# A decoder layer on one Trainium2 core: two more pairs of blocks computed with seven products, and a convolution chain in the FFN moved two weight units earlier

## The chip, the cores and the metric

The kernel runs on one core of a Trainium2 chip. A core has five engines with a queue of instructions each: TensorE (PE in the profile) multiplies matrices, VectorE (DVE) and ScalarE (ACT) do elementwise work, GpSimd (POOL) and SyncE (SP) do little here but start DMA transfers. An engine runs its queue in order and waits on semaphores for the work of the others. The metric is the device time of one execution in microseconds, the median of several runs.

## The reference

A decoder layer, batch 1, 256 tokens, width 2048, all in float32, with 28 inputs:

```python
hn = rmsnorm(h, norm_mix_w)
q, k, v, g_ret, xr, yr, g_a, g_b = split(hn @ w_in)      # 1024,1024,2048,2048, then 4 x 2048
q = rotary(q); k = rotary(k) * 128**-0.5                  # 8 heads of 128
ret_out = silu(g_ret) * head_groupnorm(chunkwise_retention(q, k, v))   # 8 heads of 256 values
hr = rg_lru(causal_dwconv(xr));  rnn_out = gelu(yr) * hr
merged = sigmoid(g_a) * (ret_out @ w_proj_ret) + sigmoid(g_b) * (rnn_out @ w_proj_rnn)
h = h + merged @ w_mix_out
h = h + memory_cross_attention(rmsnorm(h), rmsnorm(mem))  # 4 heads of 512, 256 memory tokens
up = causal_dwconv(rmsnorm(h) @ ffn_w_up)                 # 2048 -> 11264, 3 taps
gate, val = split(up)
h = h + (silu(gate) * val) @ ffn_w_down                   # 5632 -> 2048
out = rmsnorm(h, final_norm_w)
```

Nearly all of the work is the products with the weights, some 420 MB of them, each used once.

## The kernel before

**Products.** Float32 operands are split into two parts, hi and lo, that TensorE multiplies fast; a product of two float32 matrices is hi·hi + lo·hi + hi·lo, three TensorE products.

**The weight stream.** `weight_plan` (L65) lists the products of the whole layer in the order in which they run, and the host lays the weights out in that order in `wall`, as pieces of 1 MB: 4 row tiles of 128 by 512 columns. A *unit* is one step of TensorE on one such piece. `prefetch` (L248) prepares a unit: SP loads the piece into one of 6 buffers `raw` (L265), ScalarE casts hi (L286), VectorE takes lo = raw - hi (L287); hi and lo have 3 buffers each. `units` (L308) keeps two units prepared ahead of the one that runs. After each unit it runs the small work that has been put off by `later(n, fn)` (L304): n + 1 steps on from where it was registered. The Tile scheduler then writes out each engine's order from these program positions; blocks under `tc.high_priority(URGENT)` go ahead of their place.

**Three ways to run a block of 512 columns.** `gemm_t` (L328) keeps the weights stationary and gives features by tokens, in two accumulators; `joined` (L539) empties them (ScalarE copy L544, VectorE add L545). `gemm_n` (L371) streams the weights and gives tokens by features in one accumulator, 96 products of TensorE for 16 row tiles (L362, L363, L369). `pair_products` (L385) does two neighbouring blocks at once with seven products instead of eight (Strassen-Winograd): eight of the sixteen row tiles go through the seven units q1 to q7 of 12 products each, the rest through the plain units p0 to p3 of 24 each, 180 products in place of 192. It takes all three accumulators of the pool `pm` (xz, yu, rw). The sums of weights that it needs are made in the raw buffers, three of which it names A, B and C: q5 and q7 by an adding DMA of GpSimd (L267: A gets another piece added, later B does), and two VectorE adds (L294: A + B behind q5's lo; L292: A + C behind the lo of the unit that follows q6). q6 and q4 cast what stands in A and load nothing. The order of the units is `PAIR_UNITS` (L103): q1, p0, q3, p1, q5, q2, q6, p2, q7, q4, p3. The sums of the activations are made by `sums` (L494); `pair_out` (L445) and `pair_add` (L424) take the results out of the accumulators.

**The front.** The weight plan begins with Q, V, K, V (blocks of 512 columns each), then the retention gate as a pair; then the second half of the heads, with its two value blocks as a pair. The input, transposed by the host (`x_t`), is loaded, scaled and split while Q runs (`Pairs`, L618). The four sums for the pairs need x_t again: `sum_x` (L867) loads a tile (L870), scales it on ScalarE (L872) and makes the sums; it is called at steps 0 to 3 behind the first value block. `tables` (L691), one step behind Q, makes the rotary tables and spreads the row factors over the partitions (through TensorE, L605); `rotated` (L713) turns Q and K. `split_rows` scales and splits the value blocks.

**The FFN** runs in three parts of 4, 4 and 3 column blocks of hidden features. A block takes a gate and a value product (`up`, L1261): gemm_n, then ScalarE writes 16-bit planes, SP starts two DMA transposes (`turn_planes`, L1201; L1205), ScalarE joins the planes (`join_planes`, copies L763) and VectorE scales; `conv` (L1277) is one ScalarE and two VectorE instructions per tile of 128 features, the taps; `hidden` (L1351) makes silu(gate)·value and splits it. Each of these chains has two halves (pr = 0, 1), put off by `at` steps: (1, 2) for most blocks, (2, 4) for the last value block of parts one and two. The last value block of part three runs as gemm_t instead (`at=None`), and so needs no transpose. Then come the down products into the residual rows `hrow`: parts one and two as two pairs (`pair_add`), part three as four blocks (`down`, L1288) of 12 row tiles, the last of them split in four quarters with the final norm behind each. The sums of activations are made only for the first four halves of a paired part (L1358). SP also keeps the residual rows in DRAM between parts (`put_rows`, `get_rows`) and loads the final norm's weights (L1383).

Of the kernel before, what the change touches and what calls it, by code (L numbers as in the profile page):

```python
# [14 lines left out]
ALU = mybir.AluOpType  # L15
# [49 lines left out]
def weight_plan():  # L65

    w0 = "w_in"
    plan = []
    v, u = O_V, O_V + 1024
    plan += [(w0, 0, NT, O_Q), (w0, 0, NT, v), (w0, 0, NT, O_K), (w0, 0, NT, v + BW), (w0, 0, NT, O_G, O_G + BW)]  # L70
    plan += [(w0, 0, NT, O_Q + BW), (w0, 0, NT, u, u + BW), (w0, 0, NT, O_K + BW)]
    plan += [(w0, 0, NT, O_G + 1024, O_G + 1024 + BW)]
    for b in range(4):
        plan += [(w0, 0, NT, c + b * BW) for c in (O_XR, O_YR)]
    for w, c, pairs in ((w0, O_GA, (0, 2)), (w0, O_GB, (0,)), ("w_proj_ret", 0, (0, 2))):
        plan += [(w, 0, NT, c + b * BW, c + (b + 1) * BW) for b in pairs]
        if len(pairs) == 1:
            plan += [(w, 0, NT, c + b * BW) for b in (2, 3)]
    plan += [("w_proj_rnn", 0, NT, b * BW) for b in range(4)]
    plan += residual_plan("w_mix_out")  # L80
    plan += [(w, 0, NT, b * BW, (b + 1) * BW) for w in ("xa_w_q", "xa_w_k") for b in (0, 2)]
    plan += residual_plan("xa_w_v")
    plan += residual_plan("xa_w_o")
    b0 = 0
    for nb_ in FF_PARTS:
        for b in range(b0, b0 + nb_):
            plan += [("ffn_w_up", 0, NT, c + b * BW) for c in (0, FF)]
        if nb_ == 4:
            plan += [("ffn_w_down", b0 * BW, NT, b * BW, (b + 1) * BW) for b in (0, 2)]
        else:  # L90
            plan += [("ffn_w_down", b0 * BW, 4 * nb_, b * BW) for b in range(4)]
        b0 += nb_
    return plan

# [20 lines left out]
]  # L115


def entry_units(e):

    w, row, nk, cols = e[0], e[1], e[2], e[3:5]  # L120
    if len(cols) == 1:
        return [("p", None, "new", (w, tuple(row + (k + i) * P for i in range(KC)), cols[0])) for k in range(0, nk, KC)]
    out = []
    for kind, slot, a in PAIR_UNITS:
# [30 lines left out]
def hybrid_layer(  # L155
# [148 lines left out]
    def later(n, fn):  # L304

        pending.append((step[0] + n + 1, fn))
# [75 lines left out]
                lower_n(a[:, tt, :], ops[tt], parts, k0 + KC >= nk)  # L382
        return a

    def pair_products(w, row, st, ss, c0, c1, out):  # L385
# [19 lines left out]
        e = (w, row, NT, c0, c1)  # L405
# [18 lines left out]
    def pair_add(w, row, st, ss, c0, c1, h0, h1):  # L424

        def add(o, i, op=ALU.add):
            dve.tensor_tensor(out=o, in0=o, in1=i, op=op)  # L427

        def out(kind, x, z, yu, rw):
            if kind == "q1":  # L430
                add(h0[:, 0, :], x)
            elif kind == "q5":
                later(3, lambda: add(h1, rw))
                later(4, lambda: add(h1, z[:, None, :].to_broadcast([P, 2, BW])))
            elif kind == "q6":
                add(h1[:, 0, :], x, ALU.subtract)
            elif kind == "q7":
                add(h0[:, 1, :], x)
                add(h1[:, 1, :], x, ALU.subtract)
            elif kind == "p3":  # L440
                add(h0, yu)

        pair_products(w, row, st, ss, c0, c1, out)

    def pair_out(w, st, ss, c0, r=None):  # L445

# [435 lines left out]
    for g in range(2):  # L882
        dec = big([P, 4, S], s="dec")
        vs, turned = [], []
        for b, o in enumerate((O_Q, O_K)):
            a = qjoin if g == b == 0 else [joined(t, "q") for t in gemm_t("w_in", 0, xs, NT, o + g * BW)]
            if b == 0:
                sp.dma_start(
                    out=dec,
                    in_=consts[:, C_DEC + g * 4 * S : C_DEC + (g + 1) * 4 * S].rearrange("p (h s) -> p h s", s=S),  # L890
                )
            if g > 0:
                turned.append(rotated(a))
                if b == 0:
                    vs += [split_rows(v, rs0) for v in pair_out("w_in", xs, xs_sums, O_V + 1024)]
            else:
                if b == 1:
                    turned.append(rotated(a))
                v = gemm_n("w_in", 0, xs, NT, O_V + b * BW)
                if b == 0:  # L900
# [360 lines left out]
    def up(c0, b, at, then):  # L1261

        if at is None:
            for pr, a in enumerate(gemm_t("ffn_w_up", 0, h2s, NT, c0 + b * BW)):
                then(pr, scaled(a, "uz"))
            return
        d = turn_planes(row_planes(gemm_n("ffn_w_up", 0, h2s, NT, c0 + b * BW)))

        def turned(pr):
            z = join_planes(d, pr)  # L1270
            dve.tensor_tensor(out=z, in0=z, in1=rsb2, op=ALU.mult)
            then(pr, z)

        for pr in range(2):
            later(at[pr], lambda pr=pr: turned(pr))
# [72 lines left out]
            hrow[b] = big([P, 2, BW], s="nat")  # L1348
            sp.dma_start(out=hrow[b], in_=fkept[n, b])

    def hidden(gt, vl, pr, summed):  # L1351
# [11 lines left out]
    for part, nb_ in enumerate(FF_PARTS):  # L1363
# [3 lines left out]
        for b in range(b0, b0 + nb_):  # L1367
# [6 lines left out]
            def finish_up(pr, z, b=b, gt=gt, vl=vl, paired=paired):  # L1374
                conv(FF, b, pr, z, vl)
                hidden(gt, vl, pr, paired)
# [56 lines left out]
```

## Time and profile before

| | |
|---|---|
| median of 3 runs | 1997.59 us (1996.73 to 1998.44) |
| the profiled execution, its own time | 1995.6 us |
| its span, first to last instruction | 1993.8 us |
| TensorE busy | 1968.6 us (99%), 9304 products |
| VectorE busy | 1566.4 us (79%) |
| ScalarE busy | 1277.2 us (64%) |
| GpSimd busy | 43.2 us (2%) |
| mean granted TensorE clock | 0.995 |
| moved by DMA | 456.59 MB, mean 229 GB/s |

The profile is of one execution, which lies 2.0 us below the median. PE is TensorE's products, PEld its weight loads, which overlap them; a queue's own steps carry a q (SPq). "L287 DVE ... lo<-raw,hi x420 | 950.9, 2267" is a group of instructions: line 287, on VectorE, writing lo from raw and hi, 420 of them, 950.9 us in all, 2267 ns each; what follows is the idle time of the engine just ahead of them and what ended it. The granted clock is the share of full speed at which TensorE ran in a stretch. A page of averages says little about single places, so most of the reading is of stretches of 2 to 40 us.

### The profile page before, as it was taken

To read this page: it belongs to the slowest core of one execution; us is meant where nothing else is said; L and a number is where in the kernel's file an instruction comes from. 1 tells how busy PE (TensorE), PEld (TensorE's weight loads), DVE (VectorE), ACT (ScalarE), POOL (GpSimd) and SP (SyncE) were. 2 spreads that over 40 slices of the span, in tenths; PEclk is the share of its full clock that TensorE was granted. 3 is DMA by queue.
4 is the path that set the end of the run, shared out by engine and by line. 5 is a ranking of instruction groups with operands and counts; after the bars stand their busy time and mean duration, and the time that the engine had idled before them with its cause. 6 is when DMAs were issued, how large, how long until landed. Compare 5 with 4: busy or idle time off the path is not lost.

```text
span 1993.8 us, 23634 instructions
## 1 busy us (share of the span) xinstructions
PE 1968.6 (99%) x9304; PEld 1650.8 (83%) x9304; DVE 1566.4 (79%) x1546; ACT 1277.2 (64%) x1323; POOL 43.2 (2%) x52
## 2 busy tenths in 40 slices
PE   9999999999999999999999999999989999899998
PEld 7888888888888888888888888888878888788887
DVE  6978888889886886779988778677786777885775
ACT  6655656767677554567778756567744667546662
POOL 0000000000000000000000000000000000000000
PEclk9999999999999999999999999999999999899999
DMA  9675674655887865878998748766777677686671
GB/s 369 233 261 147 223 264 161 230 190 160 266 260 220 248 250 190 252 256 258 270 259 235 267 125 271 236 226 204 234 232 273 207 219 236 204 278 228 211 245 61
DMA packets 146463, 456.59 MB, mean 229 GB/s; under 512 B 77744, under 2 KB 82480, under 8 KB 98608
## 3 DMA queue, kind: packets, MB, share of 16 engines
q1 hardware_dynamic: 139072, 410.51, 58.7%
q0 software_dynamic: 5760, 41.95, 11.6%
q10 hardware_dynamic: 1520, 2.63, 0.4%
q8 instruction: 73, 1.20, 0.2%
q14 instruction: 38, 0.31, 0.0%
HBM read 420.96 MB, written 16.78 MB: 220 GB/s over the span
## 4 chain that ended last, share of the span: by engine, by line
PE 91%; DVE 4%; ACT 2%; DMA 1%; issue 1%; SPq 0%; POOLq 0%; ACTq 0%; DVEq 0%
PE acc L362 25%; PE acc L363 25%; PE acc L369 24%; PE acc L351 14%; PE sm L518 2%; DVE lo L287 1%; ACT hi L286 1%; DMA raw<-in_wall 1%; PE acc L518 1%; PE sm L948 1%; PE sm L532 1%; DVE raw L294 0%; DVE fv L1283 0%; DMA d<-rp 0%; DVE tb L722 0%
## 5 line engine op out<-in xcount | busy, mean ns | idle before, releaser
L287 DVE TENSOR_TENSOR lo<-raw,hi 128x2048 fp32r<-128x2048 f32 (+1 forms) x420 | 950.9, 2267 | 297.8 <-ACT hi L286 297.0
L286 ACT CAST hi<-raw 128x2048 fp32r<-128x2048 f32 (+1 forms) x418 | 793.2, 1901 | 522.7 <-PE acc L363 374.8
L362 PE MATMUL acc<-hi,s 128*128 128x512 f32 x2008 | 787.3, 392 | 12.4 <-ACT hi L286 12.3
L363 PE MATMUL acc<-hi,s 128*128 128x512 f32 x2008 | 784.3, 391 | 0.0
L369 PE MATMUL acc<-lo,s 128*128 128x512 f32 x2008 | 501.1, 389 | 0.0
L362 PEld LDWEIGHTS acc<-hi,s 128*128 128x128 f32 x2008 | 378.6, 189 | 91.5 <-ACT hi L286 13.2
L363 PEld LDWEIGHTS acc<-hi,s 128*128 128x128 f32 x2008 | 378.9, 189 | 78.5 <-DVE s L556 1.0
L369 PEld LDWEIGHTS acc<-lo,s 128*128 128x128 f32 x2008 | 377.1, 188 | 78.3
L351 PE MATMUL acc<-s,hi 128*128 128x512 f32 x832 | 200.4, 392 | 2.1 <-DVE hi L284 1.5
L351 PEld LDWEIGHTS acc<-s,hi 128*128 128x128 f32 x832 | 153.5, 188 | 32.8 <-issue 1.6
L362 PE MATMUL acc<-hi,ss 128*128 128x512 f32 x320 | 125.8, 393 | 0.8 <-ACT o L454 0.6
L363 PE MATMUL acc<-hi,ss 128*128 128x512 f32 x320 | 124.7, 390 | 0.0
L763 ACT COPY jp<-d 128x512 uint16<-128x512 uint16 x132 | 93.4, 771 | 29.4 <-DMA d<-rp 29.3
L351 PEld LDWEIGHTS acc<-s,lo 128*128 128x128 f32 x832 | 107.1, 191 | 4.9 <-DVE lo L287 1.3
L351 PE MATMUL acc<-s,lo 128*128 128x256 f32 x832 | 110.5, 284 | 0.5 <-DVE lo L287 0.5
L369 PE MATMUL acc<-lo,ss 128*128 128x512 f32 x320 | 85.6, 389 | 0.0
L362 PEld LDWEIGHTS acc<-hi,ss 128*128 128x128 f32 x320 | 60.1, 188 | 14.5 <-ACT o L454 1.4
L369 PEld LDWEIGHTS acc<-lo,ss 128*128 128x128 f32 x320 | 60.1, 188 | 12.6
L363 PEld LDWEIGHTS acc<-hi,ss 128*128 128x128 f32 x320 | 60.1, 188 | 12.2
L267 POOL DMA_DIRECT2D raw<-in_wall x40 | 35.2, 880 | 1550.7 <-DVE lo L287 887.5
L427 DVE TENSOR_TENSOR nat<-nat,acc 128x512 f32<-128x512 f32 (+1 forms) x49 | 44.0, 910 | 14.9 <-PE acc L369 14.9
L292 DVE TENSOR_TENSOR raw<-raw,raw 128x2048 f32<-128x2048 f32 x20 | 45.8, 2288 | 0.4
(235 smaller groups left out, 1251.7 us busy)
## 6 DMA issues: line engine op xcount, KB each, us to landing
raw<-in_wall SPq DMA_DIRECT2D x333, 1024.0 KB, 5.0
raw<-in_wall POOLq DMA_DIRECT2D x40, 1024.0 KB, 8.2
fkept<-nat SPq DMA_DIRECT2D x12, 512.0 KB, 7.7
nat<-fkept SPq DMA_DIRECT2D x12, 512.0 KB, 5.6
xt<-in_x_t SPq DMA_DIRECT2D x11, 256.0 KB, 7.8
raw<-in_wall SPq DMA_DIRECT2D x5, 512.0 KB, 7.9
nat<-in_x ACTq DMA_DIRECT2D x4, 512.0 KB, 10.1
ret<-hr SPq DMA_DIRECT2D x4, 512.0 KB, 4.6
```

The source lines that it names most:

```text
L267: pool.dma_start(out=raw, in_=src, accum_op=ALU.add)
L286: act.copy(hi[:, a:b], raw[:, a:b])
L287: dve.tensor_tensor(out=lo[:, a:b], in0=raw[:, a:b], in1=hi[:, a:b].bitcast(F32), op=ALU.subtract)
L292: dve.tensor_tensor(out=to, in0=to, in1=by, op=ALU.add)
L351: pe.matmul(a, part, sx, start=k == 0 and t == 0, stop=k == nk - 1 and t == 0, skip_group_check=True)
L362: pe.matmul(o, h, hi, start=start and kk == 0, stop=False, skip_group_check=True)
L363: pe.matmul(o, l, hi, start=False, stop=False, skip_group_check=True)
L369: pe.matmul(o, h, lo, start=False, stop=stop and kk == KC - 1, skip_group_check=True)
L427: dve.tensor_tensor(out=o, in0=o, in1=i, op=op)
L518: ins = pe.matmul(o, a, b, start=start and i == 0, stop=stop and i == 2, skip_group_check=True)
L532: ins = pe.transpose(t[:, j, tt * P : (tt + 1) * P], rows[:, tt, k + j * P : k + (j + 1) * P], ident)
L763: ins = act.copy(words(t)[:, :, :, 1 - i], d[:, i, 2 * pr : 2 * pr + 2, :])
```

## The change

Three parts, in one diff.

1. The first two value blocks of the front become a pair of seven products, and the order of the plan becomes Q, K, value pair, gate pair. `sum_x` is now called at steps 0 to 3 behind Q, that is during K; Q is rotated at step 1 and K at step 8 of what follows, during the value pair. The load of the decay tables `dec` moves ahead of the block.
2. The first two down blocks of the FFN's last part become a pair too. They have 12 row tiles, so eight go through q1 to q7 and four through p0 and p1 only, in an order of their own (`SHORT_PAIR_UNITS`); the two blocks' results are finished together behind it. The sums of activations are now made in this part too. Blocks 2 and 3 stay as they were.
3. In parts one and two the last value block's halves both run two steps behind the block, in place of two and four, and their whole chain (join, scale, convolution, hidden, sums) is under high priority.

```diff
@@ weight_plan
-    plan += [(w0, 0, NT, O_Q), (w0, 0, NT, v), (w0, 0, NT, O_K), (w0, 0, NT, v + BW), (w0, 0, NT, O_G, O_G + BW)]
+    plan += [(w0, 0, NT, O_Q), (w0, 0, NT, O_K), (w0, 0, NT, v, v + BW), (w0, 0, NT, O_G, O_G + BW)]
...
-            plan += [("ffn_w_down", b0 * BW, 4 * nb_, b * BW) for b in range(4)]
+            plan += [("ffn_w_down", b0 * BW, 4 * nb_, 0, BW)]
+            plan += [("ffn_w_down", b0 * BW, 4 * nb_, b * BW) for b in (2, 3)]
+SHORT_PAIR_UNITS = [
+    ("q1", "A", ("new", 0, 0)),
+    ("q3", "B", ("new", 1, 1)),
+    ("q2", "C", ("new", 1, 0)),
+    ("p0", None, (1, 8)),
+    ("q5", "A", ("add", 0, 1)),
+    ("p1", None, (0, 8)),
+    ("q6", "A", ("sum",)),
+    ("q7", "B", ("add", 0, 1)),
+    ("q4", "A", ("sum",)),
+]
@@ pair_add (nk is passed on to pair_products)
+            short = nk < NT
             if kind == "q1":
                 add(h0[:, 0, :], x)
             elif kind == "q5":
-                later(3, lambda: add(h1, rw))
-                later(4, lambda: add(h1, z[:, None, :].to_broadcast([P, 2, BW])))
+                later(0 if short else 3, lambda: add(h1, rw))
+                later(1 if short else 4, lambda: add(h1, z[:, None, :].to_broadcast([P, 2, BW])))
...
-            elif kind == "p3":
+            elif kind == ("q4" if short else "p3"):
                 add(h0, yu)
@@ the front, for g in range(2)
-        for b, o in enumerate((O_Q, O_K)):
-            a = qjoin if g == b == 0 else [joined(t, "q") for t in gemm_t("w_in", 0, xs, NT, o + g * BW)]
...
-            if g > 0:
-                turned.append(rotated(a))
-                if b == 0:
-                    vs += [split_rows(v, rs0) for v in pair_out("w_in", xs, xs_sums, O_V + 1024)]
-            else:
-                if b == 1:
-                    turned.append(rotated(a))
-                v = gemm_n("w_in", 0, xs, NT, O_V + b * BW)
-                if b == 0:
-                    turned.append(rotated(a))
-                    for i in range(KC):
-                        later(i, lambda i=i: sum_x(i))
-                vs.append(split_rows(v, rs0))
...
+        if g == 0:
+            for i in range(KC):
+                later(i, lambda i=i: sum_x(i))
+            for n, a in ((1, qjoin), (8, block(O_K))):
+                later(n, lambda turned=turned, a=a: turned.append(rotated(a)))
+            value_rows()
+        else:
+            turned.append(rotated(block(O_Q)))
+            value_rows()
+            turned.append(rotated(block(O_K)))
@@ up
         def turned(pr):
-            z = join_planes(d, pr)
-            dve.tensor_tensor(out=z, in0=z, in1=rsb2, op=ALU.mult)
+            with tc.high_priority(URGENT if at[0] == at[1] else 0):
+                z = join_planes(d, pr)
+                dve.tensor_tensor(out=z, in0=z, in1=rsb2, op=ALU.mult)
             then(pr, z)
@@ the FFN
-        if summed and len(hid_sums) < KC:
+        if len(hid_sums) < KC:
             hid_sums.append(sums(o, 0.5))
...
-            up(FF, b, None if last and not paired else (2, 4) if last else (1, 2), finish_up)
+            def finish_last(pr, z, finish_up=finish_up):
+                with tc.high_priority(URGENT):
+                    finish_up(pr, z)
+
+            if last and paired:
+                up(FF, b, (2, 2), finish_last)
+            else:
+                up(FF, b, None if last else (1, 2), finish_up)
...
-            for b in range(4):
+            pair_add("ffn_w_down", b0 * BW, hid, hid_sums, 0, BW, hrow[0], hrow[1], 4 * nb_)
+            for b in range(2):
+                finish(b)
+            for b in (2, 3):
                 down(b0, hid, b, final)
```

More of the change, by code (lines that the diff above doesn't have):

```diff
@@ L123, in entry_units @@
     out = []
-    for kind, slot, a in PAIR_UNITS:
+    for kind, slot, a in PAIR_UNITS if nk == NT else SHORT_PAIR_UNITS:
         if kind[0] == "p":
@@ L383, in gemm_n, with pair_products @@
         return a
-    def pair_products(w, row, st, ss, c0, c1, out):
+    def pair_products(w, row, st, ss, c0, c1, out, nk=NT):
         xz, yu, rw = acc(), acc(), acc()
@@ L404, in pair_products @@
         names = {"q1": "x", "q2": "y", "q3": "r", "q4": "u", "q5": "z", "q6": "x", "q7": "x"}
-        e = (w, row, NT, c0, c1)
+        e = (w, row, nk, c0, c1)
         for kind, parts in units(*e):
@@ L422, in pair_products, with pair_add @@
                 out(kind, x, z, yu, rw)
-    def pair_add(w, row, st, ss, c0, c1, h0, h1):
+    def pair_add(w, row, st, ss, c0, c1, h0, h1, nk=NT):
         def add(o, i, op=ALU.add):
@@ L439, in out @@
                 add(h1[:, 1, :], x, ALU.subtract)
-            elif kind == "p3":
+            elif kind == ("q4" if short else "p3"):
                 add(h0, yu)
-        pair_products(w, row, st, ss, c0, c1, out)
+        pair_products(w, row, st, ss, c0, c1, out, nk)
     def pair_out(w, st, ss, c0, r=None):
@@ L884, in hybrid_layer, with block, value_rows @@
         vs, turned = [], []
-        for b, o in enumerate((O_Q, O_K)):
-            a = qjoin if g == b == 0 else [joined(t, "q") for t in gemm_t("w_in", 0, xs, NT, o + g * BW)]
-            if b == 0:
[L888 to L891, printed above, removed]
-            if g > 0:
-                turned.append(rotated(a))
-                if b == 0:
-                    vs += [split_rows(v, rs0) for v in pair_out("w_in", xs, xs_sums, O_V + 1024)]
-            else:
-                if b == 1:
-                    turned.append(rotated(a))
-                v = gemm_n("w_in", 0, xs, NT, O_V + b * BW)
-                if b == 0:
-                    turned.append(rotated(a))
-                    for i in range(KC):
-                        later(i, lambda i=i: sum_x(i))
-                vs.append(split_rows(v, rs0))
+        sp.dma_start(
+            out=dec,
+            in_=consts[:, C_DEC + g * 4 * S : C_DEC + (g + 1) * 4 * S].rearrange("p (h s) -> p h s", s=S),
+        )
+        def block(o):
+            return [joined(t, "q") for t in gemm_t("w_in", 0, xs, NT, o + g * BW)]
+        def value_rows():
+            vs.extend(split_rows(v, rs0) for v in pair_out("w_in", xs, xs_sums, O_V + g * 1024))
+        if g == 0:
[8 more added lines that the diff above has]
+            turned.append(rotated(block(O_K)))
         qr, kr = turned
@@ L1349, in get_rows, with hidden @@
             sp.dma_start(out=hrow[b], in_=fkept[n, b])
-    def hidden(gt, vl, pr, summed):
+    def hidden(gt, vl, pr):
         cs = slice(2 * pr, 2 * pr + 2)
@@ L1372, in hybrid_layer, with finish_up @@
                 later(0, lambda part=part, n=2 if paired else 4: get_rows(part % 2, range(n)))
-            def finish_up(pr, z, b=b, gt=gt, vl=vl, paired=paired):
+            def finish_up(pr, z, b=b, gt=gt, vl=vl):
                 conv(FF, b, pr, z, vl)
-                hidden(gt, vl, pr, paired)
-            up(FF, b, None if last and not paired else (2, 4) if last else (1, 2), finish_up)
+                hidden(gt, vl, pr)
+            def finish_last(pr, z, finish_up=finish_up):
[5 more added lines that the diff above has]
+                up(FF, b, None if last else (1, 2), finish_up)
         if final:
```

## The prediction

> **What bounds the kernel now.** I read the page's first and fifth parts, then stretches whose ends I set where TensorE changes from one weight block to the next, then the waits, the chain and the timeline at the four places that the change touches.
>
> ```profile
> span 1993.8 us, 23634 instructions
> PE 1968.6 (99%) x9304; PEld 1650.8 (83%) x9304; DVE 1566.4 (79%) x1546; ACT 1277.2 (64%) x1323; POOL 43.2 (2%) x52
> L287 DVE TENSOR_TENSOR lo<-raw,hi 128x2048 fp32r<-128x2048 f32 (+1 forms) x420 | 950.9, 2267 | 297.8 <-ACT hi L286 297.0
> L286 ACT CAST hi<-raw 128x2048 fp32r<-128x2048 f32 (+1 forms) x418 | 793.2, 1901 | 522.7 <-PE acc L363 374.8
> ```
>
> TensorE sets the time; each unit of 1 MB of weights also costs ScalarE 1.9 us (hi cast) and VectorE 2.3 us (lo).
>
> ```profile
> core 0: us, PE busy (x) PEld busy (x) DVE busy (x) ACT busy (x) POOL busy (x), PEclk, DMA share, GB/s
> 30.28:52.55 22.27, 22.27 (x103) 18.48 (x101) 15.33 (x22) 14.94 (x23) 0.71 (x1) 1.00 1.00 401
> 52.55:74.77 22.22, 22.22 (x130) 19.69 (x129) 20.66 (x28) 13.89 (x18) 0.00 (x0) 1.00 0.79 306
> 74.77:96.55 21.78, 21.78 (x98) 18.03 (x97) 19.00 (x25) 13.22 (x15) 1.04 (x1) 1.00 0.46 148
> 96.55:137.35 40.80, 40.80 (x181) 33.79 (x180) 33.71 (x20) 24.13 (x18) 0.87 (x1) 1.00 0.80 258
> 1456.66:1476.05 19.39, 13.32 (x49) 10.21 (x48) 15.97 (x16) 8.51 (x8) 0.00 (x0) 0.82 0.73 277
> 1720.85:1741.35 20.50, 14.22 (x49) 10.81 (x48) 16.30 (x16) 8.72 (x8) 0.00 (x0) 0.75 0.68 261
> 1918.61:1951.78 33.17, 33.07 (x147) 26.89 (x145) 25.10 (x28) 18.11 (x19) 0.00 (x0) 1.00 0.51 189
> ```
>
> In order: first value block (96 products and a spread), first key block, second value block, first gate pair; the last units of the first down pair of FFN parts one and two; the last part's first two down blocks. A pair of seven products takes 40.80 us for 180 products: 0.227 us a product, 2.72 us for a unit q of 12, 5.44 us for a unit p of 24. So TensorE starves only where the two FFN rows stand: 48 products should take 10.88 us and took 19.39 and 20.50, a loss of 8.5 and 9.6 us, 18.1 in all. The chain shows what they wait for:
>
> ```profile
> 1444.21 2.30 DVE raw L294
> 1447.15 8.09 DMA raw<-in_wall
> 1455.34 1.92 ACT hi L286
> 1457.26 0.51 ACT fv L1281
> 1458.28 1.27 DVE fv L1283 x3
> 1459.55 2.21 DVE raw L292
> 1461.84 1.91 ACT hi L286
> 1463.79 1.33 PE acc L362 x2
> ```
>
> VectorE's sum A+B frees B, GpSimd's adding transfer into B takes 8.1 us, q7's cast waits for it, and behind that cast in ScalarE's queue stands the last value block's convolution; the sum for q4 stands behind its taps. A wait costs more than its length:
>
> ```profile
> 1457.60:1463.70 6.10, 0.13 (x1) 0.00 (x0) 5.99 (x8) 2.51 (x4) 0.00 (x0) 0.81 0.58 199
> 1463.70:1468.00 4.30, 4.21 (x10) 3.00 (x11) 4.25 (x4) 0.57 (x2) 0.00 (x0) 0.50 0.98 408
> 1470.00:1472.00 2.00, 2.00 (x11) 1.65 (x10) 0.73 (x1) 1.41 (x1) 0.00 (x0) 1.00 1.04 430
> ```
>
> After it the granted clock is 0.50 and ten products take 4.3 us instead of 2.3: about 2.1 us more.
>
> **The change, part by part.** *Products.* Two value blocks are 192 products, a pair 180; the last part's two down blocks (12 row tiles) are 144, the short pair 132. Each saves 12 x 0.227 = 2.7 us, 5.4 in all, if nothing waits. Added: nine units of casts for eight (full pair) or nine for six (short), two VectorE sums and two adding transfers each, more result adds.
>
> *First value pair.* Q, K, then the pair, instead of Q, V, K, V. The four reloads of x_t (and their sums) now fall in K's block, and K's two accumulators must be emptied before the pair's second unit, p0, as there are three accumulators and the pair takes three. In the changed program's order ScalarE empties them behind the scaling of the fourth reload; SP issues that reload behind the weight load of the gate pair's q1, which reuses p1's weight buffer and so waits for p1's lo; p1's hi cast needs the buffer of q1's, so it cannot come before TensorE runs q1.
>
> ```profile
> 52.87 1.28 ACT L702 ACT_TABLE_LOAD   x1
> 54.16 0.42 ACT L702 ACTIVATE sin<-rot 128x256 f32<-128x256 f32 x1
> 69.10 1.02 SPq L870 DMA_DIRECT2D xt<-in_x_t  x1
> 69.35 0.90 ACT L872 ACTIVATE xt<-xt,pa 128x256 f32<-128x256 f32 x2
> 81.81 1.05 ACT L544 COPY c<-acc 128x512 f32<-128x512 f32 x2
> 84.03 1.28 DVE L545 TENSOR_TENSOR q<-acc,c 128x512 f32<-128x512 f32 x2
> DMA to landing us min/median/max: 5.3/7.8/11.0
> ```
>
> (The last row is of the x_t reloads.) Counted from K's end: q3's cast ends at +1.0 (its buffer, of K's last unit, is free at -0.9); table load, sine, cosine to +3.1; second reload's scaling +4.0; p1's hi +5.9, lo +8.2; two issues +8.8; landing, 5.3 by the reload with least before it, +14.1; scaling +15.0; two copies +16.0; second add +16.6. q1 is done at +2.7, so TensorE waits 13.9 us (19.6 with the longest landing). Half clock then: 2.1. The spread of the row factors is queued behind the reload's sums and two lo's, about 1.3 us late by the same walk (between 0 and 2). VectorE, with two rotations and the pair's sums, is some 0.8 us late for the gate pair. Together 13.9 + 2.1 + 1.3 + 0.8 - 2.7 = +15.4; the ends are -2.7 (all hidden) and +21.
>
> *Last value blocks moved up* (parts one and two). In the new order the pair's second half still stands behind q7's cast on ScalarE, so the 8.1 us transfer still leads; what changes is that the sum for q4 goes ahead of the taps (1.8 us sooner), while VectorE puts the lo's of q2, q6 and p2 ahead of the first half's products. Bounds: 0 and the whole 18.1. I take 2.0 each, nearest to the 1.8 that leaves the path: -4.0.
>
> *Last part.* The SP queue holds one more weight load ahead of the gate block's transposes; it reuses the buffer of the value block's last unit, whose lo ends at 1904.5.
>
> ```profile
> 1902.19 2.29 DVE L287 TENSOR_TENSOR lo<-raw,hi 128x2048 fp32r<-128x2048 f32 x1 [2.57 <-ACT hi L286]
> 1899.47 5.05 SPq L1205 DMA_TRANSPOSE d<-rp  x2
> 1906.74 1.40 ACT L763 COPY jp<-d 128x512 uint16<-128x512 uint16 x2 [4.61 <-DMA d<-rp]
> 1922.74 1.66 DVE L1283 SCALAR_TENSOR_TENSOR fv<-uz,pf,fv 128x255 f32<-128x255 f32 x4
> 1918.74 0.68 DVE L545 TENSOR_TENSOR uz<-acc,c 128x512 f32<-128x512 f32 x1
> 1447.15 0.89 POOL L267 DMA_DIRECT2D raw<-in_wall  x1 [21.87 <-DVE fv L1283]
> ```
>
> So the transposes go from 1899.5 to 1904.7 and land at 1912. Then: four copies 1914.9; q3's hi 1916.7, lo 1918.9; eight gate taps 1922.1; three small operations 1923.9; q2's lo 1926.1; four taps 1927.7; the add that empties the value block's second accumulator 1928.3. The short pair's second unit, q3, writes into that accumulator's buffer; q1 ends at 1918.6 + 2.7 = 1921.3, so TensorE waits 7.0 us, and runs q3 at half clock to 1933.1. q5's cast waits for q3's buffer (1933.8), and behind it on ScalarE stand the second half's tanh, split and convolution and p1's cast (1937.9). VectorE then has taps, two small operations, p0's lo, the split, q5's and p1's lo (1946.0), then A+B (1948.2); the adding transfer lands 8.7 later, 1956.9; q7's cast ends 1958.8. TensorE is through q6 at 1953.8 and waits 5 us; q7 and q4, part of it at half clock, end near 1966.3 instead of 1951.8: +14.5 (ends: -2.7 if nothing is late, +17 with the slowest adding transfer here). If the transposes were on time VectorE would be 5 us earlier and most of it gone. Nothing after it recovers: two blocks and a tail that TensorE sets.
>
> The idle rule behind the half clock is in the Trainium skill, "TensorE: Matmul & The Clock Gate", section "HAM oscillation — how this bites in real kernels": idle gaps over about 3.4 us put TensorE back to half clock. It speaks against this change, and the rows above agree (0.50 after 6.1 us). The page's 1.67 us of throttled time would make a wait 0.8 us dearer, not 2.1, an estimate by which the sum would be about 4 us lower, 2018.
>
> *Sum*: +15.4 + 14.5 - 4.0 = +25.9 on the profiled execution's 1995.6: 2021.5; that one lies 2.0 under the median of 1997.59, on which it is 2023.5. I say 2022.
>
> **The rivals.** *First wait hidden*: if K's accumulators are emptied when K ends, the first part is -2.7: 2023.5 - 18.1 = 2005. For it: in the run before, the copies at 81.8 stood in nobody's way; against it: the order of the two queues. *Last wait hidden*: transposes early enough, -2.7 instead of +14.5: 2006. Against it: the buffer's lo ends after 1904. *Faster*: the chain that the change moves gets ahead of q7's cast, so that the 18.1 us go, and the pairs wait for nothing: 1997.6 - 18.1 - 5.4 = 1974 (1988 if only the pairs are clean). It decides at one point: whether the fourth reload lands before K ends, some 14 us sooner than I count. *No change*: one pair waits half as long and the FFN gain is whole: near 1998. *Worse*: reload at 11 us, no FFN gain: over 2031.
>
> **How the numbers follow.** Forecast 0.60 (2012 to 2031), first hidden 0.12, last hidden 0.13, faster 0.05, no change 0.05, worse 0.05. The range 2003 to 2031 leaves out the last three. 0.2% (4 us) is about what a measurement of this kernel can tell: faster 0.05, same 0.05, slower 0.90.
>
> **What would show it.** In the changed kernel: a TensorE wait of 12 to 20 us after the first 12 products of the value pair, ended by the add that empties K's accumulator, with granted clock 0.50 behind it; near 1933 (1921.3 + 15.4 - 4.0) a wait after the short pair's first 12 products and another ahead of q7; transposes issued 5 us later; the two old FFN waits still there, 1 to 3 us shorter. I am wrong if ScalarE's copies of K's accumulators come right at K's end, or if the two FFN waits are gone.

## The result, and the profile after

| | before | changed |
|---|---|---|
| median | 1997.16 us | 2019.78 us |
| shortest to longest run | 1995.49 to 1998.44 | 2019.29 to 2020.46 |
| span of the profiled execution | 1993.8 us | 2018.4 us |

The changed kernel is slower by 22.6 us: ratio 1.0114, 95% interval 1.0102 to 1.0126. The forecast was 2022. First the page of the changed kernel: span, busy time by engine, and the two groups of weight preparation.

```profile
span 2018.4 us, 23664 instructions
...
PE 1972.5 (98%) x9280; PEld 1651.8 (82%) x9280; DVE 1602.2 (79%) x1585; ACT 1292.8 (64%) x1337; POOL 46.7 (2%) x56
...
L301 DVE TENSOR_TENSOR lo<-raw,hi 128x2048 fp32r<-128x2048 f32 (+1 forms) x426 | 964.5, 2268 | 287.8 <-ACT hi L300 284.7
L300 ACT CAST hi<-raw 128x2048 fp32r<-128x2048 f32 (+1 forms) x424 | 803.7, 1901 | 510.6 <-PE acc L377 361.5
```

There are 24 products fewer, and VectorE works 35.8 us more. TensorE's share fell to 98%: it waits. What it waits for (engine, line, releaser: us in total, times, longest):

```profile
PE acc L376 <- DVE q L560: 14.2, 1, 14.2
PE acc L376 <- ACT hi L300: 10.9, 4, 4.2
PE acc L376 <- DVE uz L560: 4.6, 2, 3.6
PE acc L377 <- DVE s L571: 3.7, 3, 1.9
```

The first row is the wait for K's accumulators in the value pair; the second the two FFN ends and the short pair's q7; the third the short pair's q3 and q2; the fourth again mostly the FFN ends, which wait for the split of the hidden features. The stretches where they lie, in the columns of the prediction: K, the first unit of the value pair with its wait, the rest of that pair, the gate pair, the front as a whole; then the first down pair of FFN part one, its two waits (1.9 and 3.2 us) with the few products around them, and what follows; then q1 of the short pair with its wait, q3 with its own, and the short pair as a whole.

```profile
30.93:54.79 23.86, 22.96 (x134) 20.16 (x133) 16.75 (x26) 15.31 (x26) 1.74 (x2) 1.00 1.02 380
54.79:71.87 17.08, 2.92 (x15) 2.11 (x13) 10.50 (x20) 9.81 (x15) 0.00 (x0) 0.71 0.68 248
71.87:111.74 39.87, 39.87 (x168) 32.85 (x169) 39.48 (x37) 23.61 (x19) 1.49 (x2) 0.95 0.48 159
111.74:152.54 40.80, 40.80 (x181) 33.78 (x180) 36.99 (x22) 25.31 (x20) 1.13 (x2) 1.00 0.85 261
30.93:152.54 121.61, 106.54 (x494) 88.91 (x493) 103.73 (x103) 74.05 (x78) 4.36 (x5) 0.94 0.74 249
...
1448.14:1497.49 49.35, 44.18 (x181) 35.70 (x180) 40.67 (x35) 29.28 (x26) 1.73 (x2) 0.93 0.68 204
1472.62:1479.14 6.52, 1.35 (x5) 0.49 (x4) 6.52 (x10) 4.77 (x5) 0.00 (x0) 0.94 0.55 182
1479.14:1483.15 4.01, 4.01 (x10) 3.15 (x10) 4.01 (x4) 0.63 (x1) 0.00 (x0) 0.50 0.74 282
...
1932.68:1939.16 6.48, 2.91 (x14) 2.08 (x12) 6.10 (x11) 6.48 (x9) 0.00 (x0) 1.00 1.00 312
1939.16:1944.84 5.68, 4.60 (x13) 3.40 (x13) 5.68 (x9) 3.97 (x6) 0.00 (x0) 0.70 0.24 100
1932.68:1976.74 44.06, 34.69 (x134) 26.75 (x133) 40.89 (x43) 25.16 (x25) 0.86 (x1) 0.92 0.59 184
```

VectorE (third busy time) is at 99% in the rest of the value pair (39.48 of 39.87) and at 93% in the whole short pair, but at 61% in the value pair's first unit with its wait, and at 85% in the front as a whole. The front in the kernel before, and its last three stretches (last gate block, last value block, down blocks 0 and 1), with the changed kernel's behind:

```profile
30.28:137.35 107.07, 107.07 (x506) 89.99 (x505) 88.69 (x94) 66.19 (x71) 2.61 (x3) 1.00 0.77 275
1874.63:1951.78 77.15, 77.05 (x370) 64.59 (x368) 56.01 (x61) 48.28 (x53) 0.00 (x0) 1.00 0.67 231
```

```profile
1888.70:1976.74 88.04, 78.67 (x357) 64.44 (x356) 71.69 (x83) 54.24 (x54) 1.73 (x2) 0.96 0.67 201
```

Each new pair takes twelve products away from TensorE, 2.7 us, and gives VectorE 15.0 us (front, 88.69 to 103.73) and 15.7 us (last part, 56.01 to 71.69) more to do: three more lo's of 2.3 us, two sums of weights of 2.3, result adds; in the last part the four sums of activations too.

The chain of the front in the changed kernel, from the third reload to p0 (start, length, what):

```profile
58.95 0.04 ACT xt L887
...
59.36 0.49 ACT xt L887
59.85 1.80 ACT hi L300
...
61.68 2.29 DVE lo L301
63.97 0.21 DVE sm L519
64.18 0.14 SPq L279
...
64.37 5.11 DMA xt<-in_x_t
...
69.56 0.92 ACT xt L887 x2
...
71.12 0.61 DVE q L560
...
71.87 0.77 PE acc L376
```

It is the chain of the forecast: cast and lo of p1, the weight load that waits for that lo, the fourth reload behind it on SP, its scaling on ScalarE, and only then K's accumulators. The reload landed 14.7 us after K's end (69.48 - 54.79); 14.1 were forecast.

### The profile page after: what moved, and what is told of

It reads as the page before. It is cut to its first block, busy times and chain, and to the rows that moved or that the text cites. A ratio compares the mean times of both kernels' runs of the same rounds, so it can differ in the third digit from the quotient of the medians.

```text
span 2018.4 us, 23664 instructions
## 1 busy us (share of the span) xinstructions
PE 1972.5 (98%) x9280; PEld 1651.8 (82%) x9280; DVE 1602.2 (79%) x1585; ACT 1292.8 (64%) x1337; POOL 46.7 (2%) x56
## 4 chain that ended last, share of the span: by engine, by line
PE 88%; DVE 5%; DMA 4%; ACT 2%; issue 1%; SPq 0%; POOLq 0%; ACTq 0%; DVEq 0%
PE acc L376 25%; PE acc L377 24%; PE acc L383 24%; PE acc L365 11%; DVE lo L301 2%; PE sm L533 2%; DMA xt<-in_x_t 1%; DMA raw<-in_wall 1%; ACT hi L300 1%; PE acc L533 1%; DMA d<-rp 1%; PE sm L964 1%; PE sm L547 1%; DMA nat<-in_x 0%; DVE fv L1300 0%
## 5 line engine op out<-in xcount | busy, mean ns | idle before, releaser
L301 DVE TENSOR_TENSOR lo<-raw,hi 128x2048 fp32r<-128x2048 f32 (+1 forms) x426 | 964.5, 2268 | 287.8 <-ACT hi L300 284.7
L300 ACT CAST hi<-raw 128x2048 fp32r<-128x2048 f32 (+1 forms) x424 | 803.7, 1901 | 510.6 <-PE acc L377 361.5
L376 PE MATMUL acc<-hi,s 128*128 128x512 f32 x1968 | 772.4, 393 | 21.9 <-DVE q L560 14.2
L377 PE MATMUL acc<-hi,s 128*128 128x512 f32 x1968 | 769.5, 391 | 3.7 <-DVE s L571 3.7
L383 PE MATMUL acc<-lo,s 128*128 128x512 f32 x1968 | 491.4, 389 | 0.0
L376 PEld LDWEIGHTS acc<-hi,s 128*128 128x128 f32 x1968 | 371.7, 189 | 100.3 <-issue 16.0
L377 PEld LDWEIGHTS acc<-hi,s 128*128 128x128 f32 x1968 | 371.4, 189 | 81.3 <-DVE s L571 5.0
L383 PEld LDWEIGHTS acc<-lo,s 128*128 128x128 f32 x1968 | 369.3, 188 | 76.6
L376 PE MATMUL acc<-hi,ss 128*128 128x512 f32 x352 | 141.2, 401 | 8.5 <-ACT hi L300 4.2
L377 PE MATMUL acc<-hi,ss 128*128 128x512 f32 x352 | 139.6, 397 | 0.0
L383 PE MATMUL acc<-lo,ss 128*128 128x512 f32 x352 | 94.2, 389 | 0.0
L376 PEld LDWEIGHTS acc<-hi,ss 128*128 128x128 f32 x352 | 67.7, 192 | 24.9 <-ACT hi L300 4.6
L377 PEld LDWEIGHTS acc<-hi,ss 128*128 128x128 f32 x352 | 67.8, 193 | 14.0
L441 DVE TENSOR_TENSOR nat<-nat,acc 128x512 f32<-128x512 f32 (+1 forms) x56 | 50.3, 910 | 13.5 <-PE acc L383 13.4
```

The costliest lines, as they stand in the source:

```text
L300: act.copy(hi[:, a:b], raw[:, a:b])
L301: dve.tensor_tensor(out=lo[:, a:b], in0=raw[:, a:b], in1=hi[:, a:b].bitcast(F32), op=ALU.subtract)
L376: pe.matmul(o, h, hi, start=start and kk == 0, stop=False, skip_group_check=True)
L377: pe.matmul(o, l, hi, start=False, stop=False, skip_group_check=True)
L383: pe.matmul(o, h, lo, start=False, stop=stop and kk == KC - 1, skip_group_check=True)
```

## The experiments

To compare stretches across kernels I take their lengths from the starts of TensorE's units in each trace: the front from the end of Q to the end of the gate pair, the first down pair of FFN parts one and two, and down blocks 0 and 1 of the last part. The rest of the span is 1753.6 to 1757.3 us in all fourteen traces, so nothing else changes but for scatter.

| kernel | front | pair, part 1 | pair, part 2 | last, 0 and 1 | median |
|---|---|---|---|---|---|
| before | 107.1 | 49.3 | 50.4 | 33.2 | 1997.2 |
| changed | 121.6 | 49.4 | 48.5 | 44.1 | 2019.8 |
| e1 front back | 107.1 | 46.9 | 47.5 | 43.4 | 2002.5 |
| e2 last back | 121.8 | 46.8 | 48.0 | 34.2 | 2008.7 |
| e3 ends back | 122.3 | 50.6 | 50.7 | 44.1 | 2024.6 |
| e4 reloads early | 120.7 | 48.5 | 47.7 | 43.6 | 2015.0 |
| e5 transposes first | 121.3 | 46.8 | 48.0 | 45.3 | 2021.7 |
| e6 plain q7 | 122.6 | 48.0 | 50.4 | 44.1 | 2021.0 |
| e7 no taps | 123.5 | 42.7 | 45.2 | 43.9 | 2014.3 |
| e8 GpSimd in the front | 122.3 | 46.6 | 50.8 | 43.7 | 2018.8 |
| e9 ends alone | 107.1 | 46.9 | 47.7 | 33.2 | 1993.1 |
| e10 no rotation | 116.0 | 47.9 | 48.7 | 43.7 | 2012.7 |
| e11 last without taps | 124.2 | 48.1 | 51.4 | 40.9 | 2015.7 |
| e12 scaled rows | 107.1 | 41.8 | 41.8 | 33.3 | 1981.6 |

The same code scatters from trace to trace: the changed front from 121.3 to 124.2, the moved-up ends from 46.6 to 49.4 and 47.5 to 51.4. So a difference of 3 to 4 us between two single traces decides nothing by itself; without the change the front took 107.1 in all four traces. (For e11 the last column counts the 132 products of the pair; four products of the next block run among them and are left out.)

### Each part undone (e1, e2, e3)

```diff
 e1: the front
-    plan += [(w0, 0, NT, O_Q), (w0, 0, NT, O_K), (w0, 0, NT, v, v + BW), ...
+    plan += [(w0, 0, NT, O_Q), (w0, 0, NT, v), (w0, 0, NT, O_K), (w0, 0, NT, v + BW), ...
+    (and the loop over g of the kernel before)
 e2: the last part
-            pair_add("ffn_w_down", b0 * BW, hid, hid_sums, 0, BW, hrow[0], hrow[1], 4 * nb_)
...
+            for b in range(4):
+                down(b0, hid, b, final)
 e3: the ends of parts one and two
-                up(FF, b, (2, 2), finish_last)
+                up(FF, b, (2, 4), finish_up)
```

> The changed kernel with the front of the kernel before (Q, V, K, V, the reloads behind the first value block). Theory: the front's cost is local, 14.5 us between the end of Q and the second half of the heads in the two traces (66.3 us before, 80.8 after), and nothing later gives any of it back: 2019.8 - 14.5 = 2005.3 (2004 to 2007). Rival: later parts have slack that a slower front uses up, so that taking it back gives less: 2009 or more.

> The changed kernel with the four plain down blocks of the kernel before in the last FFN part. Theory: blocks 0 and 1 took 33.2 us before and 44.1 after, so 10.9 us go: 2008.9 (2008 to 2010). Rival: the sums of activations, casts and adds that the pair brings also cost the blocks ahead of it or the tail behind it, so that more goes: 2006 or less.

> The changed kernel with the last value blocks of parts one and two put off by two and four steps again and without the raised priority. The two down pairs ahead of which this stands took 49.3 and 50.4 us before and 49.4 and 48.5 after. Theory: the move is worth what these show, 0 and 1.9 us: 2019.8 + 1.9 = 2021.7 (2019.5 to 2023). Rival (the move is worth the 2.0 us each of the forecast, and the traces show scatter): 2023.8 or more.

Measured: 2002.5 (below the range expected), 2008.7 and 2024.6: the front costs 17.3 us, the last part 11.0, the moved-up ends gain 4.8. Together 23.5, against 22.6 for the whole: the parts add up. The front's 17.3 is more than the 14.5 of the one trace; over the seven traces that have this front unchanged (changed, e2, e3, e5, e6, e7, e11) it took 122.5 us on average, 15.4 more than before. No slack later gives any of it back. For e3 the rival was right: the first trace had shown the moved-up ends at their slowest. Over all traces with the moved-up chain and nothing else changed there they took 47.5 and 48.7 us on average, 2.4 and 1.8 us less than with the old placing (two traces, 50.0 and 50.5).

### The front: early reloads (e4)

```diff
     def sum_x(i):
-        t = tmp("xt")
-        sp.dma_start(out=t, in_=x_t[:, 2 * i : 2 * i + 2, :])
+        while len(xs_again) < (KC if i else 1):
+            k = len(xs_again)
+            t = big([P, 2, BW], s="xt")[:, :, 0:S]
+            sp.dma_start(out=t, in_=x_t[:, 2 * k : 2 * k + 2, :])
+            xs_again.append(t)
+        t = xs_again[i]
```

> The changed kernel with its value pair and its order, but the second, third and fourth reload of x_t are issued together, ahead of the weight loads that wait for buffers, into buffers of the larger pool. Theory (the reload queued behind a weight load holds ScalarE, and with it the copies that empty K's accumulators): the fourth reload lands before K ends, the wait of 14.3 us ahead of p0 falls to 0 to 2 us and the 1.8 us at half clock go with it; the earlier reloads may cost K up to 1.5 us: 2005 (2003 to 2007). Rival (VectorE and ScalarE have too much to do at this place in any case: sums, two rotations, the pair's own sums): a wait of 6 us or more stays, with half clock behind it: 2010 or more.

Measured: 2015.0, in the rival's range, though the wait that is left is shorter than the rival's 6 us. K, the value pair's first unit, the rest of that pair and the gate pair:

```profile
32.29:57.17 24.88, 23.18 (x134) 20.13 (x133) 16.17 (x36) 19.49 (x36) 1.84 (x2) 1.00 1.02 391
57.17:63.68 6.51, 2.91 (x14) 2.10 (x13) 6.47 (x10) 5.60 (x7) 0.00 (x0) 0.93 0.99 282
63.68:104.61 40.93, 40.93 (x168) 33.63 (x169) 37.65 (x34) 21.80 (x16) 0.87 (x1) 0.93 0.57 184
104.61:152.95 48.34, 43.87 (x181) 34.58 (x180) 40.41 (x25) 25.67 (x21) 1.75 (x2) 0.96 0.65 199
```

The wait of 14.3 us is down to 3.8 (6.51 - 2.72), so the chain through the fourth reload was the last link. But the gate pair behind, 40.80 us in the changed kernel and before, now takes 48.34. VectorE had caught up during the long wait; without it, it is late for the next pair: it is still at K's rotation when the gate pair begins (104.61), a lo follows, the adding transfer is issued behind that lo (107.83), and ScalarE's next cast waits 5.9 us for it, to 118.59. The whole front is 1 us shorter in this trace. (The median is 4.8 us lower; the profiled execution was the longest of four.)

### Less work for VectorE in the front (e8, e10)

```diff
 e8, on e4: the sums of x and the rotation of the first Q on GpSimd
-        xs_sums.append(sums(t))
+        xs_sums.append(sums(t, eng=pool))
...
+    later(n, lambda ..., e=pool if n == 1 else dve: turned.append(rotated(a, e)))
 e10, on e4: no rotation of the first Q and K
+            if not turn:
+                o.append(split_pair(q))
+                continue
```

> The kernel with the early reloads, in which GpSimd does the sixteen small subtractions and additions of the four sums of x and the multiplications and additions of the rotation of the first Q (on VectorE 4.6 and 5.5 us). With the early reloads alone the wait ahead of p0 fell from 14.3 to 3.8 us, but the gate pair behind took 48.3 us in place of 40.8. Theory (the front is paid on VectorE: 88.7 us of its work before, 103.7 after, whatever waits last): with 10 us of work less the waits that are left shrink, 2015.0 - 7 = 2008 (2004 to 2011). Rival (the order of the queues at each place, not the amount of work): 2013 or more.

> The kernel with the early reloads, without the rotation of the first Q and the first K (it leaves out the rotary embedding of the first four heads, 11 us of multiplications and additions on VectorE; the splits stay). With the early reloads the front from the end of Q to the end of the gate pair took 120.7 us, 107.1 in the kernel before. Theory (the pair's price is work on VectorE): most of the 11 us come back: 2015.0 - 9 = 2006 (2003 to 2009). Rival (the order at each place): 2012 or more.

Measured: 2018.8 and 2012.7; by their medians both went to the rivals. The stretches say more. K, first unit, rest of the value pair and gate pair in e10:

```profile
30.04:58.29 28.25, 24.78 (x134) 21.25 (x133) 18.56 (x37) 20.34 (x36) 1.84 (x2) 0.94 1.03 387
58.29:64.20 5.91, 2.91 (x14) 2.10 (x13) 5.88 (x10) 5.65 (x8) 0.00 (x0) 0.93 0.90 269
64.20:105.19 40.99, 40.99 (x168) 33.67 (x169) 32.89 (x21) 22.23 (x17) 1.73 (x2) 0.93 0.62 190
105.19:145.99 40.80, 40.80 (x181) 33.78 (x180) 35.45 (x21) 25.36 (x20) 0.89 (x1) 1.00 0.78 250
```

Without the rotations the two pairs take 87.7 us (5.91 + 40.99 + 40.80) in place of e4's 95.8: 8.1 us for 11 us of VectorE's work, and the gate pair is whole again. There, in one trace of each (e10's was the shortest of its four, e4's the longest), the theory holds. The median fell by 2.4 us only. In the trace K itself got longer, 28.25 us in place of e4's 24.88 and of 23.86 in the changed kernel. With early reloads ScalarE scales x ahead of the squares for the row factors, and behind those stand the spread of the factors on TensorE (L620) and the cast of K's third unit: the cast began at 40.43 in the changed kernel, at 43.89 in e4, 43.59 in e8 and 43.41 in e10. TensorE waited for the spread 0.9 us in the changed kernel, 1.7 in e4, 3.6 in e8 and 3.5 in e10, where Q ended 2 us earlier than in e4, and ran at half clock behind the last two. Not all of this is the early reloads: with the changed kernel's own front e7 and e11 waited 2.4 and 3.1 us there, and K took 26.9 and 27.3.

In e8 the gate pair was whole too (40.80), but the value pair took 52.3 us in place of e4's 47.4 (6.51 + 40.93), and K 29.1. It shows a second price. While GpSimd works beside it, VectorE's own instructions get longer; between 63 and 90 us, by group in e8 and in e4:

```profile
L737 DVE TENSOR_TENSOR tb<-q,sin 64x512 f32<-64x512 f32 x2 | 3.3, 1674 | 0.0
L735 DVE TENSOR_TENSOR ta<-q,cos 128x512 f32<-128x512 f32 x2 | 2.5, 1229 | 0.0
```

```profile
L737 DVE TENSOR_TENSOR tb<-q,sin 64x512 f32<-64x512 f32 x4 | 2.7, 686 | 0.1
L735 DVE TENSOR_TENSOR ta<-q,cos 128x512 f32<-128x512 f32 x2 | 1.4, 688 | 0.0
```

The Trainium skill, "SBUF — State Buffer", section "Terms", says that VectorE and GpSimd arbitrate for a shared pair of ports, locked for a whole instruction, and that the loser stands still. The trace agrees in what it shows: 0.69 us became 1.67 and 1.23; the lock itself it does not show. VectorE was busy for 101.5 us of e8's front and 100.7 of e4's, so work moved to GpSimd was not work taken from VectorE.

### The ends of FFN parts one and two (e6, e7)

```diff
 e6, in prefetch, for q7 of the first down pair of parts one and two
+            if taken[0] in alone:
+                slot, op = None, "new"
 e7, for the last value block of parts one and two
-            for s in range(1, 3):
+            for s in range(1, 3) if taps else ():
```

> The changed kernel, in which q7 of the first down pair of parts one and two multiplies its newly loaded piece alone, from a buffer of its own: no adding transfer into B, nothing that q7's cast waits for. It leaves the sum B + piece out of q7 in these two units. Theory A (the 8.1 us of the adding transfer and the cast behind it lead to the wait at the end of q6): the two waits of 6.5 us with their half clock go, some 8 us each: 2004 (2002 to 2008). Theory B (VectorE is full from the end of the up blocks on, and the transfer is only just in time): under 2 us each: 2016 to 2020.

> The changed kernel without the two taps of the convolution on VectorE in the last value block of parts one and two (it leaves out those taps, eight instructions of 0.47 us in each part; ScalarE's scale and bias stay). Theory A (the adding transfer leads): 1 us each at most: 2018 or more. Theory B (VectorE's amount of work leads): each wait ends some 3.8 us sooner and its half clock is shorter: 2012 (2009 to 2014).

Measured: 2021.0 and 2014.3. Theory A falls: with nothing to wait for, q7's cast comes at the same place, 24.4 us into the pair in e6 and 24.5 in the changed kernel. In the kernel before ScalarE had stood 2.4 us ahead of that cast for the transfer (to 1455.34); in the changed kernel it no longer does. In e6 ScalarE stands 2.4 us ahead of the split (L577), because VectorE is late with the product (L1380), and comes to q7's cast (L307) at 1472.87, where the changed kernel had it at 1472.62:

```profile
1471.18 0.63 ACT L577 ACTIVATE s<-fo 128x512 fp32r<-128x512 f32 x1 [2.43 <-DVE fo L1380]
...
1472.87 1.89 ACT L307 CAST hi<-raw 128x2048 fp32r<-128x2048 f32 x1
```

In e7, with 3.8 us less for VectorE in each part, the two pairs took 42.7 and 45.2 us, 5 and 3.5 us less than the averages. That is theory B, with a median 0.3 us outside its range.

### The last part (e5, e11)

```diff
 e5, in prefetch, for p1 of the short pair and the unit behind it
+                        with tc.issue_after(turned_last[0].ins):
+                            sp.dma_start(out=raw[:, a:b, :], in_=src[:, a:b, :])
 e11, for the last block of part three
-            for s in range(1, 3):
+            for s in range(1, 3) if taps else ():
```

> The changed kernel with the load of the short pair's p1 queued behind the last gate block's transposes on SP, not ahead of them; nothing else of the order moves but a few instructions on VectorE and ScalarE behind it. Theory (the transposes' wait for a weight buffer makes VectorE late for the short pair): they are issued some 5 us sooner, the wait ahead of q3 (3.8 us and 2.9 us more at half clock) goes and the one ahead of q7 (4.4 us) shrinks: 2012 (2009 to 2014). Rival (VectorE has more work than time there whatever comes first): both waits stay within 2 us: 2018 or more.

> The changed kernel without the taps of the convolution in the last block of part three, gate and value (it leaves out those taps, sixteen instructions of 0.41 to 0.48 us on VectorE, 6.5 us; transposes, SP's queue and the short pair are as they were). Theory (the short pair is paid on VectorE: 71.7 us of its work in the last three stretches, 56.0 before): the waits ahead of q3 and q7 shrink by 5 to 8 us in all: 2013.5 (2011 to 2016). Rival (the late transposes and the adding transfers lead): 2018 or more.

e5 measured 2021.7, the rival's side, but not as the rival said: the wait ahead of q3 did go (q1 ran on to q3 after 2.75 us), and others came behind it, of 2.8 us ahead of q2 and of 1.4 and 4.4 us further on, so that the pair took 45.3 us. The wait moved and did not go. The transposes were issued 8.8 us after the gate block's end (1918.12 and 1909.36), and 8.9 us in the changed kernel (1919.31 and 1910.46): taking the weight load out of their way made them no earlier. What they read was late itself. ScalarE's row planes (rp) in the changed kernel:

```profile
1916.69 0.64 ACT L524 ACTIVATE ss<-sm 128x512 fp32r<-128x512 f32 x1 [0.49 <-DVE sm L519]
1917.23 1.91 ACT L772 COPY rp<-acc 128x1024 uint16<-128x1024 uint16 x2
...
1919.31 5.58 SPq L1221 DMA_TRANSPOSE d<-rp  x2
```

The gate block ended at 1910.46, and rp begins 6.8 us later; before it began 0.7 us after the block's end (1897.13 and 1896.39). In between stand the sums of activations, new in this part, for which ScalarE waits on VectorE; in e2, which has neither these sums nor the pair, rp again begins 0.7 us after the block's end (1908.83 and 1908.09). e11 measured 2015.7, at the far end of the theory's range (four executions from 2012.5 to 2020.8): with 6.5 us less for VectorE the short pair took 40.9 us in place of 44.1. The stretch of q1, q3 and q2 fell by 4.5 us, but the wait ahead of q7 grew from 4.4 to 5.5, so the waits did not shrink by the 5 to 8 us expected. Two adding transfers in series, in e11 10.9 us into A and 8.2 into B, with cast, lo and sum between them, have less time in a pair of nine units than in one of eleven. How much of the short pair's price is this chain and how much VectorE stays open: no run shortened the transfers.

### The ends alone, and a faster kernel (e9, e12)

```diff
 e9: the kernel before with the third part of the change alone
 e12, on e9, for the last blocks of parts one and two
+            rows = big([P, 2, BW], s="ur")
+            for tt in range(2):
+                act.mul(rows[:, tt, :], a[:, tt, :], rs2[:, tt : tt + 1])
+            a = rows
...
+                if not by_row:
                     dve.tensor_tensor(out=z, in0=z, in1=rsb2, op=ALU.mult)
```

> The kernel before with the third part of the change alone: the last value blocks of parts one and two moved up. Theory: the three parts add up; undone in the changed kernel it cost 4.8 us, so here it gains 4: 1993 (1991 to 1995), and is faster than both kernels. Rival: its gain needs what the other parts do to the transfers: 1996 or more.

> As the third part alone, and the last gate and value block of parts one and two are scaled by the row factors on ScalarE, as rows ahead of the transposes (two instructions a block), not by two multiplications of 0.68 us a block on VectorE. Theory (VectorE's amount of work ahead of the down pairs is the limit): 2.7 us of its work go in each part, the waits get 2 us shorter each: 4 us under the third part alone, 1989 (1986 to 1992). Rival (the chain's length is the limit, and it grows by 1.2 us on ScalarE): no less than the third part alone.

e9: 1993.1 us, ratio to the kernel before 0.998 (0.9968 to 0.9992). e12: 1981.6 us, ratio 0.9917 (0.9899 to 0.9935), 15 us under the kernel before and 38 under the changed one, and three times the gain expected over e9. The first down pair of part one, first in e9, then in e12, and the stretch in e12 where the wait was:

```profile
1434.49:1481.38 46.89, 42.99 (x181) 34.72 (x180) 40.67 (x35) 29.30 (x26) 1.76 (x2) 0.96 0.68 215
```

```profile
1433.24:1475.08 41.84, 41.11 (x181) 33.71 (x180) 38.62 (x33) 30.34 (x28) 1.77 (x2) 1.00 0.74 236
1457.72:1464.20 6.48, 5.75 (x25) 4.43 (x24) 6.48 (x5) 2.74 (x3) 0.00 (x0) 1.00 0.82 283
```

Some 1.0 us of wait is left (6.48 - 5.44), and the granted clock stays 1.00. Two things came together: VectorE's 2.7 us went, and on ScalarE the second half's convolution now stands ahead of q7's cast. No run separates them. And with the wait its half clock went: e9 has waits of 0.7 and 3.2 us in this pair and a granted clock of 0.96 over it, e12 one wait and 1.00.

## Why the prediction was right or wrong

- **Front, +15.4.** Right, and by the mechanism named. Wait 14.3 us (13.9 forecast), half clock 1.8 (2.1), K 1.6 us longer with the spread in it, the gate pair not late at all (0.8); 14.5 in the trace, 15.4 over seven traces, 17.3 by e1. But the working treats the wait as the cause of the price. e4 takes 10.5 us of the wait away, and most of the price stays: 4.8 of e1's 17.3 us went by the medians. What the pair brings is 15.0 us of work on VectorE in a stretch where it had 18.4 us left (107.07 - 88.69), spread over places; e10 shows that less of this work brings time back in the two pairs. How much of the front's price is this work and how much the order of the queues in K and behind it stays open.
- **Ends of parts one and two, -4.0.** The size was right (4.8 by e3, 3.7 by e9; 1.9 between the two first traces), the reason was wrong, so the size is luck. The step that failed is "the pair's second half still stands behind q7's cast on ScalarE, so the 8.1 us transfer still leads": the place in the queue was as said, but e6 shows that the transfer does not lead any more; VectorE does (e7). The long wait ended in both kernels with q4's cast behind VectorE's sum A + C (1461.84 before, 1477.19 after); new in the changed kernel is a shorter one ahead of it, 1.9 us, for the split of the hidden features.
- **Last part, +14.5.** The sign and the places were right: 10.9 in the trace, 11.0 by e2. Mis-sized is the wait ahead of q3, 7.0 us forecast. q3 writes into the buffer that the first accumulator of the value block leaves, not the second's; its wait ended with the first add (L560, 1938.43), 3.6 us, and q2 waited 1.0 for the second. The wait ahead of q7 was 4.4 (5 forecast). The transposes were as late as said (8.3 us after the gate block's end; 8.9 measured), but the cause given, the weight load on SP, does not decide: without it (e5) they came as late, because rp itself was late behind the new sums, which the walk had left out.
- **Sum.** +25.9 forecast, 24.6 between the two spans, 22.6 between the medians. The last part's 3.6 us too many make up the difference to the medians. The list of added work has one slip that enters no term: a full pair casts eleven units for eight, not nine (27 lo's in the front for 24).
- **Half clock.** It follows the waits as forecast; p0 took 1.8 us longer after the 14.3, and q3 2.9 after the 3.6. By the Trainium skill, "TensorE: Matmul & The Clock Gate", section "HAM oscillation — how this bites in real kernels", with its 1.67 us of throttled time, it would have been 0.8 each; the rows do not agree and decide for the dearer.
- **Rivals.** "First wait hidden" gave 2005; e4 hid most of it and came to 2015. That rival overlooked that the work which the pair brings does not go with the wait.

## What to carry to other kernels

A transformation that trades products on the bounding engine for work on another one is priced in the stretch where it is made: here 2.7 us of TensorE for 15 us of VectorE, on a VectorE that the page shows 79% busy and the stretch 83%. When a wait is found, ask what the late engine does with the time after it is removed: if the engine behind it is nearly full, the wait can move and not go, as in e4 and e5. And look for the 2 or 3 us that end a wait and the half clock with it: in e12 two multiplications a block, moved to an engine with room, gave back 11.5 us over e9 (1993.1 to 1981.6), though the order on ScalarE changed with them.

## What the hardware showed that was not expected

Half clock followed short waits. In e10 p0, 5.44 us at full speed, took 8.35 behind one of 3.1 us, at a granted clock of 0.64. (The section of the Trainium skill named above speaks of gaps over about 3.4 us; here a shorter one did it, behind a K block that had itself waited.) In e4's gate pair a unit of 2.72 us took 4.45 behind a wait of only 1.9 us, with no other wait in the 14 us ahead of it. The waits of 1.0 us in e12 and of 1.7 in e4, ahead of the spread, had none behind them. These traces give no sharp length. The two rows of e10, then those of e4:

```profile
61.05:64.15 3.10, 0.15 (x1) 0.00 (x0) 3.10 (x4) 3.10 (x5) 0.00 (x0) 0.87 0.84 333
64.25:72.50 8.25, 8.25 (x24) 6.57 (x25) 4.41 (x5) 2.48 (x3) 0.00 (x0) 0.64 0.34 130
...
122.15:124.05 1.90, 0.00 (x0) 0.00 (x0) 1.90 (x2) 1.85 (x2) 0.00 (x0) 1.00 0.05 22
124.05:128.50 4.45, 4.45 (x12) 3.53 (x13) 4.45 (x3) 0.00 (x0) 0.00 (x0) 0.62 0.00 0
```

GpSimd's multiplication of two 128x512 operands took 1.65 us in e8, where VectorE's takes 0.69 in e4, and VectorE was slower meanwhile.
